# The front of a hybrid mixer: two small pieces of work given out in other projection groups

## The chip, the cores and the metric

The kernel runs on one core of one Trainium2 chip. The time is that of the device for one execution, in microseconds (us). The engines are TensorE (PE in the profile, with its weight loads as PEld), VectorE (DVE), ScalarE (ACT), GpSimd (POOL) and SyncE (SP); SP issues nearly all transfers here.

## The reference, cut to what matters

One decoder layer over 512 tokens of width 1024: an RMS norm, one input projection, whose columns feed a differential attention and an RWKV-7 time mixing, then the output projection, a product-key expert stage and a gated embedding. The change touches what stands at the front of the two mixers:

```python
u = rms_norm(h, norm_mix_g[i]);  z = u @ w_in[i]          # (512, 3328)
# time mixing: shift by one token, then keys, receptances, values, low-rank columns
zs = z_rw + (prev - z_rw) * mu
kk = heads(k * k_k)
kk = kk / jnp.maximum(jnp.sqrt(jnp.sum(kk * kk, axis=-1, keepdims=True)), 1e-12)
# attention: rotation's tables, and lambda
ang = positions[..., None] * inv_freq;  cos, sin = jnp.cos(ang), jnp.sin(ang)
lam = jnp.exp(jnp.sum(lam_q1 * lam_k1)) - jnp.exp(jnp.sum(lam_q2 * lam_k2)) + lam_init
```

## The kernel before

Tokens lie in four blocks of 128 partitions. Every float32 product is made of three matmuls: operands are split in a high part (`whi`, `uhi`, made on ACT, L133) and the rest (`wlo`, `ulo`, made on DVE, L145 where a gain is folded in, L143 elsewhere), and `proj_steps` (L217 to L219) adds high by high, high by rest and rest by high.

The front is a chain of projection groups, each of eight chunks of 128 rows of the weight: the keys "k" (512 columns), the low-rank columns "l" (256), the receptances "r" (512), the values "v" (512), and then the attention's queries, keys and values. `stream` fetches two chunks at a time into `wraw` (three buffers), and the halves of a pair of chunks share one of two buffers, so that ACT can make `whi` of a pair only when PE is done with the pair two before. A chunk is twelve matmuls, three for each block of tokens. When a group is done, `consume` of `shift_group` copies it to `zz` on ACT (L446), SP moves it by one token (L455 to L460), and POOL makes the mix with `mu` in three operations for each block (L461, L462, L464: `zs`).

`rw_keys` makes the normalised keys: the product `kk` on DVE (L475), its square on ACT (L477), the sums (L478), a reciprocal root in small steps on DVE (`rsqrt`, L94 to L103, L481) and four products (L484). `rope_tables` makes the cosine and sine tables from the positions by some 46 operations on tiles of 128x32 on DVE (L355 to L423) and two functions on ACT (L418, L424). `lambdas` makes two products on DVE (L340), an exponential on ACT (L342) and two small steps. After the values, `rw_prepare` starts with the low-rank columns: transposes, the copies `lw` and `lg` on DVE (L502, L504), then the matmuls `plw` and `pla` (L506, L510).

The order on each engine isn't that of the text: a planner goes through the program with its own costs and gives each engine the earliest work in the program's order that it believes to be ready, so that later work fills gaps; each engine then runs its queue strictly in that order. Tiles of a tag (the pages `p2`, 32 of them, hold `mu`, `zs`, `kk`, `zz` of "l" and others) are given out by the planner. `behind(i, first)` adds an edge for the planner alone: `i` stands behind `first` on its engine, without a semaphore. `last_lo`, `last_hi` and `last_z` are the latest `wlo`, `whi` and `zz` at that place in the program. `among` is a table of steps that `proj_steps` calls after the halves of a given chunk have been made and before that chunk's matmuls.

In the kernel before, `rw_keys` is called between the receptances and the values, and `rope_tables` and `lambdas` after the values.

Of the kernel before, what the change touches and what calls it, by code (L numbers as in the profile page):

```python
# [14 lines left out]
OP = mybir.AluOpType  # L15
# [7 lines left out]
RW0 = 1536  # L23
# [24 lines left out]
def bcast_row(ap, n):  # L48
    return bass.AP(tensor=ap.tensor, offset=ap.offset, ap=[[0, 128], [1, n]])
# [7 lines left out]
class Kernel:  # L57
# [274 lines left out]
    def lambdas(self, pool):  # L332
        nc, a = self.nc, self.a
        lam = pool.tile([128, 4, 64], F32, name="lam")
        for i, nme in enumerate(("lam_q1", "lam_k1", "lam_q2", "lam_k2")):
            nc.sync.dma_start(lam[:, i, :], bcast_row(a[nme], 64))
        e = pool.tile([128, 2], F32, name="lame")
        scr = pool.tile([128, 64], F32, name="lams")
        for i in range(2):
            nc.vector.scalar_tensor_tensor(scr, lam[:, 2 * i, :], 1.0, lam[:, 2 * i + 1, :], op0=OP.mult, op1=OP.mult,  # L340
                                           accum_out=e[:, i:i + 1])
        self.behind(nc.scalar.activation(e, e, AF.Exp), self.last_z)  # L342
        self.nlam = pool.tile([128, 1], F32, name="nlam")

        nc.vector.tensor_sub(self.nlam, e[:, 1:2], e[:, 0:1])
        nc.vector.tensor_scalar(self.nlam, self.nlam, -LAM_INIT, None, op0=OP.add)

    def rope_tables(self, pool, tmp):

        nc, a = self.nc, self.a  # L350
        n = NB * 8
        pi32 = tmp.tile([128, NB], I32, name="pi32")
        nc.sync.dma_start(pi32, a["positions"])
        pf = tmp.tile([128, NB], F32, name="posf")
        nc.vector.tensor_copy(pf, pi32)  # L355
        freq = tmp.tile([128, 8], F32, name="freq")
        inv = np.power(np.float32(500000.0), -np.arange(8, dtype=np.float32) * np.float32(2.0) / np.float32(16))
        for j in range(8):
# [6 lines left out]
        def f(name):  # L365
            return tmp.tile([128, n], F32, name=name)
# [52 lines left out]
        w = f("xw")  # L419
# [6 lines left out]
    def p2(self, name, shape=(128, 512), dt=F32):  # L426
        return self.pages.tile(list(shape), dt, name=name, tag="p2", bufs=32)
# [468 lines left out]
    def mixers(self, ocat_pool, psum):  # L896

        tc, nc, a = self.tc, self.nc, self.a
        w = a["w_in"]
        with ExitStack() as ctx:  # L900
# [6 lines left out]
            cpool = self.pool(ctx, "mx_const")  # L907
# [3 lines left out]
            hi = act.tile([128, KC, T], F32R, name="uhi")  # L911
            lo = act.tile([128, KC, T], F32R, name="ulo")
            g = cpool.tile([128, KC], F32, name="g_mix")
# [6 lines left out]
            def columns(k):  # L920

                xt = self.p4("xt", [128, 2, T])
                nc.sync.dma_start(xt, a["xT"][k * 128:(k + 2) * 128, :].rearrange("(k p) t -> p k t", k=2))
                self.split(hi[:, k:k + 2], lo[:, k:k + 2], xt)

            def square(b):
                x = self.p4("xb")
                nc.sync.dma_start(x, a["x"][b * 128:b * 128 + 128, :])
                self.squares(x, x, ssx[:, b:b + 1])

            def row_scales():
                self.rms(rs, ssx)

            p2, p4 = self.p2, self.p4
            zs = {}
            columns(0)
            begin = {0: [lambda: columns(2)], 2: [lambda: columns(4)], 4: [lambda: columns(6)],
                     6: [lambda b=b: square(b) for b in range(NB)] + [lambda: self.mixer_consts(cpool)],
                     7: [row_scales]}
            for tag, c0, n in (("k", 512, 512), ("l", 1536, 256), ("r", 0, 512), ("v", 1024, 512)):  # L940
                z, consume = self.shift_group(rs, (lambda: self.small.tile([128, 256], F32, name="zsl", bufs=NB))
                                              if tag == "l" else (lambda: p2("zs")), c0, n)
                if tag == "v":
                    kk = self.rw_keys(zs["k"])
                self.proj(psum, hi, lo, w, RW0 + c0, n, consume, g=g, among={} if zs else begin)
                zs[tag] = z
                if tag == MARK:
                    self.mark = self.last_hi
            self.rope_tables(cpool, cpool)
            self.lambdas(cpool)  # L950
            zd, qT, kT, vs = {}, {}, [], {}

            def eat_z(b, ps):
# [771 lines left out]
```

## Time and profile before

| | us |
|---|---|
| median of 3 runs | 1800.03 (1797.09 to 1800.13) |
| the profiled execution | 1795.69 |
| its span in the trace | 1794.0 |
| PE busy in it | 1691.8 |
| DVE busy in it | 1397.3 |
| mean granted clock of PE | 0.966 of full speed |

The times are those of one launch; the span is from the first to the last instruction that the profiler recorded. In a row of a timeline stand the start, the duration, the engine, the line of the kernel, the operation and its tiles with their sizes (out<-in), the count where rows were merged, and in brackets how long the engine had been idle and what ended that. [...]

### The profile page before, as it was taken

How to read it: one execution, taken by the hardware profiler on the slowest of the kernel's cores; microseconds unless marked ns; L12 is line 12 of the kernel's file. 1: busy time of each engine (PE TensorE's matmuls, PEld its weight loads, DVE VectorE, ACT ScalarE, POOL GpSimd, SP SyncE). 2: the span in 40 equal slices, each digit the busy share in tenths (PEclk: the TensorE clock that was granted, in tenths of full speed). 3: DMA queues.
4: the chain of work that ended last, by engine and by line, in shares of the span. 5: the costliest groups of instructions: out<-in, count | busy, mean ns of one | idle time of the engine just before them, and what ended most of it. 6: DMA issues, size and time to landing. Idle time of an engine off the chain costs nothing.

```text
span 1794.0 us, 30877 instructions
## 1 busy us (share of the span) xinstructions
PE 1691.8 (94%) x11642; PEld 1447.2 (81%) x11642; DVE 1397.3 (78%) x3004; ACT 751.5 (42%) x1358; POOL 647.3 (36%) x574
## 2 busy tenths in 40 slices
PE   7899978989889879999999999999999999999998
PEld 5767667667677879997777888888999989989986
DVE  5486858774499979878888888888888888888785
ACT  5345523343456654444444333333333333333363
POOL 3460120212278840001111233335545455555520
PEclk9899966899999989999999999999999999999999
DMA  7444353414522434455665677778989898989881
GB/s 230 147 128 118 106 130 87 111 27 165 188 82 81 139 102 132 137 188 198 210 208 190 221 267 235 262 266 299 315 301 316 301 319 301 313 308 315 304 321 47
DMA packets 150426, 363.86 MB, mean 203 GB/s; under 512 B 43922, under 2 KB 58510, under 8 KB 150148
## 3 DMA queue, kind: packets, MB, share of 16 engines
q1 hardware_dynamic: 113412, 227.65, 38.9%
q0 software_dynamic: 36864, 134.23, 22.1%
q8 instruction: 91, 1.49, 0.3%
q14 instruction: 59, 0.48, 0.1%
HBM read 332.61 MB, written 21.36 MB: 197 GB/s over the span
## 4 chain that ended last, share of the span: by engine, by line
PE 67%; DVE 24%; ACT 4%; issue 2%; DMA 2%; POOL 1%; SPq 0%; DVEq 0%; ACTq 0%; POOLq 0%
PE po L1395 22%; PE phid L1253 9%; PE phid L1255 9%; PE phid L1254 8%; PE pg L1364 3%; ACT whi L133 2%; DVE wlo L143 2%; PE acc L217 2%; PE acc L218 2%; PE acc L219 2%; DVE ids L1202 1%; DVE rest L1079 1%; DVE sol_p L630 1%; DVE wlo L145 1%; DVE jj L1352 1%
## 5 line engine op out<-in xcount | busy, mean ns | idle before, releaser
L143 DVE TENSOR_TENSOR wlo<-wraw,whi 128x1024 fp32r<-128x1024 f32 x245 | 299.6, 1223 | 144.7 <-ACT whi L133 144.6
L133 ACT ACTIVATE whi<-wraw 128x1024 fp32r<-128x1024 f32 x276 | 291.4, 1056 | 166.6 <-PE phid L1254 68.5
L1253 PE MATMUL phid<-u2dhi,whi 128*128 128x384 f32 x1024 | 349.1, 341 | 5.7 <-ACT row L1262 5.7
L1255 PE MATMUL phid<-u2dhi,wlo 128*128 128x384 f32 x1024 | 346.1, 338 | 5.5 <-POOL wlo L143 5.5
L1254 PE MATMUL phid<-u2dlo,whi 128*128 128x384 f32 x1024 | 345.6, 338 | 0.0
L1418 POOL DMA_INDIRECT row<-in_peer_u_dram,idx x128 | 190.0, 1485 | 408.0 <-DVE row L1430 219.4
L1418 POOL DMA_INDIRECT row<-in_peer_v_dram,idx x128 | 186.0, 1453 | 276.3 <-DVE h L1434 194.4
L1395 PE MATMUL po<-whi,clo 128*128 128x512 f32 x768 | 243.1, 398 | 1.4
L1395 PE MATMUL po<-whi,chi 128*128 128x512 f32 x768 | 243.3, 398 | 1.2 <-ACT row L1262 1.2
L1395 PE MATMUL po<-wlo,chi 128*128 128x512 f32 x768 | 241.4, 395 | 0.0
L1253 PEld LDWEIGHTS phid<-u2dhi,whi 128*128 128x128 f32 x1024 | 193.5, 189 | 10.8 <-ACT row L1262 6.6
L1255 PEld LDWEIGHTS phid<-u2dhi,wlo 128*128 128x128 f32 x1024 | 193.4, 189 | 6.1 <-POOL wlo L143 6.1
L1254 PEld LDWEIGHTS phid<-u2dlo,whi 128*128 128x128 f32 x1024 | 193.7, 189 | 3.7
L1395 PEld LDWEIGHTS po<-whi,clo 128*128 128x128 f32 x768 | 143.0, 188 | 41.9 <-DVE clo L145 8.7
L1395 PEld LDWEIGHTS po<-wlo,chi 128*128 128x128 f32 x768 | 144.4, 188 | 33.6
L133 ACT ACTIVATE chi<-gelu 128x384 fp32r<-128x384 f32 x128 | 67.3, 526 | 240.6 <-DVE gelu L1372 121.4
L1434 DVE SCALAR_TENSOR_TENSOR h<-row,ids,h 128x1024 f32<-128x1024 f32 x128 | 163.9, 1280 | 1.5
L1395 PEld LDWEIGHTS po<-whi,chi 128*128 128x128 f32 x768 | 140.9, 188 | 25.6 <-ACT row L1262 1.5
L1262 ACT ACTIVATE gelu<-phid 128x384 f32<-128x384 f32 x86 | 42.4, 493 | 266.4 <-PE phid L1255 244.8
L1430 DVE SCALAR_TENSOR_TENSOR row<-row,xn 128x1024 f32<-128x1024 f32 x128 | 153.6, 1219 | 0.0
L143 POOL TENSOR_TENSOR wlo<-wraw,whi 128x1024 fp32r<-128x1024 f32 (+1 forms) x46 | 80.0, 1752 | 111.3 <-ACT whi L133 111.3
L218 PE MATMUL acc<-wlo,uhi 128*128 128x512 f32 (+1 forms) x224 | 89.7, 401 | 10.7 <-DVE wlo L145 10.7
(452 smaller groups left out, 2866.1 us busy)
## 6 DMA issues: line engine op xcount, KB each, us to landing
wraw<-in_peer_uT_dram SPq DMA_DIRECT2D x128, 512.0 KB
wraw<-in_peer_v_dram SPq DMA_DIRECT2D x128, 512.0 KB
wraw<-in_w_in_dram SPq DMA_DIRECT2D x24, 512.0 KB
wraw<-in_peer_w_q_dram SPq DMA_DIRECT2D x16, 512.0 KB
ahead<-row SPq DMA_DIRECT2D x42, 192.0 KB
gelu<-ahead SPq DMA_DIRECT2D x42, 192.0 KB
wraw<-in_w_out_dram SPq DMA_DIRECT2D x8, 512.0 KB
zz<-zz SPq DMA_DIRECT2D x12, 224.0 KB
```

The costliest lines, as they stand in the source:

```text
L133: self.last_hi = nc.scalar.activation(hi, src, AF.Copy, **({} if g is None else {"scale": g}))
L143: self.last_lo = eng.tensor_tensor(lo[s], src[s], hi[s].bitcast(F32), op=OP.subtract)
L218: nc.tensor.matmul(o, hi[:, k, s], wlo, start=False, stop=False)
L1253: nc.tensor.matmul(ps, whi[:, s], hi[:, k, :], start=(k == 0), stop=False)
L1254: nc.tensor.matmul(ps, whi[:, s], lo[:, k, :], start=False, stop=False)
L1255: nc.tensor.matmul(ps, wlo[:, s], hi[:, k, :], start=False, stop=(k == KC - 1))
L1262: nc.scalar.activation(g, ps, AF.Gelu)
L1364: nc.tensor.matmul(ps[:, t], jj[:, t], gi[:, i, t], start=i == 0, stop=i == 1)
L1395: nc.tensor.matmul(outs[b, e], lhs[:, s], rhs[:, 512 * e:512 * e + 512], start=(c == 0 and rhs is vhi and lhs is chi), stop=(c == NKEY - 1 ...
L1418: nc.gpsimd.indirect_dma_start(out=row, out_offset=None, in_=a["peer_u" if kind == "U" else "peer_v"], in_offset=bass.IndirectOffsetOnAxis ...
L1430: nc.vector.scalar_tensor_tensor(row, row, 1.0, xn0, op0=OP.mult, op1=OP.mult, accum_out=hid0[:, k:k + 1])
L1434: nc.vector.scalar_tensor_tensor(acc0, row, hid0[:, k:k + 1], acc0, op0=OP.mult, op1=OP.add)
```

## The change

`rw_keys` is no longer called between the receptances and the values, but inside the receptances' group, after the halves of chunk 4. `rope_tables` and `lambdas` are no longer called after the values, but inside the values' group, after the halves of chunk 1. The first DVE operation of the tables (`posf`) and the two products of lambda are put behind the latest `wlo` at that place, which is that of chunk 1 of the values; before they had no such edge.

```diff
@@ -337,8 +337,8 @@
         e = pool.tile([128, 2], F32, name="lame")
         scr = pool.tile([128, 64], F32, name="lams")
         for i in range(2):
-            nc.vector.scalar_tensor_tensor(scr, lam[:, 2 * i, :], 1.0, lam[:, 2 * i + 1, :], op0=OP.mult, op1=OP.mult,
-                                           accum_out=e[:, i:i + 1])
+            self.behind(nc.vector.scalar_tensor_tensor(scr, lam[:, 2 * i, :], 1.0, lam[:, 2 * i + 1, :], op0=OP.mult,
+                                                       op1=OP.mult, accum_out=e[:, i:i + 1]), self.last_lo)
         self.behind(nc.scalar.activation(e, e, AF.Exp), self.last_z)
         self.nlam = pool.tile([128, 1], F32, name="nlam")
 
@@ -352,7 +352,7 @@
         pi32 = tmp.tile([128, NB], I32, name="pi32")
         nc.sync.dma_start(pi32, a["positions"])
         pf = tmp.tile([128, NB], F32, name="posf")
-        nc.vector.tensor_copy(pf, pi32)
+        self.behind(nc.vector.tensor_copy(pf, pi32), self.last_lo)
         freq = tmp.tile([128, 8], F32, name="freq")
         inv = np.power(np.float32(500000.0), -np.arange(8, dtype=np.float32) * np.float32(2.0) / np.float32(16))
         for j in range(8):
@@ -932,7 +932,7 @@
                 self.rms(rs, ssx)
 
             p2, p4 = self.p2, self.p4
-            zs = {}
+            zs, kk = {}, []
             columns(0)
             begin = {0: [lambda: columns(2)], 2: [lambda: columns(4)], 4: [lambda: columns(6)],
                      6: [lambda b=b: square(b) for b in range(NB)] + [lambda: self.mixer_consts(cpool)],
@@ -940,14 +940,13 @@
             for tag, c0, n in (("k", 512, 512), ("l", 1536, 256), ("r", 0, 512), ("v", 1024, 512)):
                 z, consume = self.shift_group(rs, (lambda: self.small.tile([128, 256], F32, name="zsl", bufs=NB))
                                               if tag == "l" else (lambda: p2("zs")), c0, n)
-                if tag == "v":
-                    kk = self.rw_keys(zs["k"])
-                self.proj(psum, hi, lo, w, RW0 + c0, n, consume, g=g, among={} if zs else begin)
+
+                among = {"k": begin, "r": {4: [lambda: kk.extend(self.rw_keys(zs["k"]))]},
+                         "v": {1: [lambda: self.rope_tables(cpool, cpool), lambda: self.lambdas(cpool)]}}
+                self.proj(psum, hi, lo, w, RW0 + c0, n, consume, g=g, among=among.get(tag, {}))
                 zs[tag] = z
                 if tag == MARK:
                     self.mark = self.last_hi
-            self.rope_tables(cpool, cpool)
-            self.lambdas(cpool)
             zd, qT, kT, vs = {}, {}, [], {}
 
             def eat_z(b, ps):
```

## Rows read from the trace of the kernel before

**Rows 1.** The page, part 1: engine, busy us, share of the span, instructions.

```profile
PE 1691.8 (94%) x11642; PEld 1447.2 (81%) x11642; DVE 1397.3 (78%) x3004; ACT 751.5 (42%) x1358; POOL 647.3 (36%) x574
```

**Rows 2.** PE in order of time: start, us, engine, line, operation, [idle before <-releaser].

```profile
33.42 0.28 PE L217 MATMUL acc<-whi,uhi 128*128 128x256 f32 x1
...
39.22 0.28 PE L217 MATMUL acc<-whi,uhi 128*128 128x256 f32 x1
42.95 0.38 PE L218 MATMUL acc<-wlo,uhi 128*128 128x256 f32 x1 [3.46 <-DVE wlo L145]
...
55.13 0.58 PE L218 MATMUL acc<-wlo,uhi 128*128 128x256 f32 x1 [7.23 <-DVE wlo L145]
...
82.38 0.39 PE L217 MATMUL acc<-whi,uhi 128*128 128x512 f32 x1
...
111.10 1.56 PE L506 MATMUL plw<-w_up,lw 65*128 65x512 f32 x2 [3.97 <-DVE lw L502]
```

**Rows 3.** Stretches of the front: busy us (instructions) by engine, PEclk, DMA share, GB/s.

```profile
43.00:47.00 4.00, 4.00 (x21) 4.00 (x22) 4.00 (x8) 0.91 (x2) 3.84 (x4) 0.57 0.62 193
...
55.20:60.50 5.30, 5.30 (x23) 5.11 (x24) 1.73 (x4) 2.12 (x5) 0.00 (x0) 0.50 0.38 121
...
82.40:104.80 22.40, 22.40 (x98) 17.88 (x97) 17.17 (x15) 9.25 (x16) 18.45 (x12) 1.00 0.46 146
...
111.00:118.50 7.50, 7.40 (x15) 4.66 (x16) 5.38 (x11) 1.46 (x3) 6.66 (x5) 0.54 0.32 81
```

**Rows 4.** DVE in order of time, 31 to 92 us.

```profile
35.81 1.27 DVE L394 TENSOR_SCALAR h<-h 128x32 f32<-128x32 f32 x1
...
42.42 1.89 DVE L145 SCALAR_TENSOR_TENSOR wlo<-wraw,g_mix,whi 128x256 fp32r<-128x256 f32 x2
...
52.15 0.18 DVE L387 SCALAR_TENSOR_TENSOR x<-x0q,x 128x32 f32<-128x32 f32 x1
...
54.59 0.88 DVE L145 SCALAR_TENSOR_TENSOR wlo<-wraw,g_mix,whi 128x256 fp32r<-128x256 f32 x2
...
78.91 1.41 DVE L145 SCALAR_TENSOR_TENSOR wlo<-wraw,g_mix,whi 128x512 fp32r<-128x512 f32 x2 [2.96 <-ACT whi L133]
```

**Rows 5.** POOL in order of time, 20 to 130 us.

```profile
35.59 1.45 POOL L461 TENSOR_TENSOR zz<-zz 128x512 f32<-128x512 f32 x1 [27.27 <-DMA zz<-zz]
...
50.88 1.29 POOL L464 TENSOR_TENSOR zs<-zz 128x512 f32<-128x512 f32 x1
...
85.40 1.29 POOL L461 TENSOR_TENSOR zz<-zz 128x512 f32<-128x512 f32 x1 [12.43 <-DMA zz<-zz]
```

**Rows 6.** DVE from 88 to 114 us: groups by line, then the first in time.

```profile
L145 DVE SCALAR_TENSOR_TENSOR wlo<-wraw,g_mix,whi 128x512 fp32r<-128x512 f32 x6 | 8.8, 1478 | 3.6 <-ACT whi L133 3.6
L475 DVE TENSOR_TENSOR kk<-zs,b_rw_k_k 128x512 f32<-128x512 f32 x4 | 5.9, 1497 | 0.0
L478 DVE TENSOR_REDUCE knr<-ksq 128x8 f32<-128x512 f32 x4 | 2.6, 676 | 0.1
L484 DVE TENSOR_TENSOR kk<-kk,knx 128x512 f32<-128x512 f32 x4 | 2.5, 684 | 0.0
...
91.58 3.46 DVE L475 TENSOR_TENSOR kk<-zs,b_rw_k_k 128x512 f32<-128x512 f32 x2
```

**Rows 7.** SP's issues in order of time, then one of ACT.

```profile
40.22 4.49 SPq L169 DMA_DIRECT2D wraw<-in_w_in_dram  x3
44.76 0.46 SPq L438 DMA_DIRECT2D mu<-in_rw_mu_dram  x1
...
92.11 0.46 SPq L438 DMA_DIRECT2D mu<-in_rw_mu_dram  x1
...
43.32 0.91 ACT L133 ACTIVATE whi<-wraw,g_mix 128x256 fp32r<-128x256 f32 x2 [5.83 <-DMA wraw<-in_w_in_dram]
```

**Rows 8.** ACT in order of time, 100 to 115 us.

```profile
106.15 1.28 ACT L418 ACT_TABLE_LOAD   x1
...
113.11 1.32 ACT L133 ACTIVATE whi<-wraw,g_mix 128x512 fp32r<-128x512 f32 x2
```

## The prediction

> **What bounds the kernel now.** I read the page first: PE is busy for 94% of the span [rows 1], so only its holes are worth anything, and the change lies in the front, before 130 us. So I read that stretch alone: PE in order of time for its holes, then a table by stretches for the clock, then DVE, POOL, ACT and SP in order of time for what fills or ends each hole. Every hole of PE over 1 us between 10 and 130 us is in [rows 2]: 3.46 us and 7.23 us in the low-rank group "l", both ended by DVE's wlo (L145), and 3.97 us at plw, ended by DVE's copy lw (L502). Each is followed by a stretch at a lower granted clock [rows 3]: 0.57 over 4.0 us, 0.50 over 5.3 us and 0.54 over 7.5 us. [...] What such a stretch costs I take as its length times what is missing from 1.00: 1.7, 2.65 and 3.45 us. PE works through all of it, so this is time of the end.
>
> What fills the holes: DVE's queue is in order, and between the wlo of "l" stand the 42 small steps of the rotation's tables, 25 of them between 35.81 and 52.15 us [rows 4]. POOL runs the keys' shift at that time (twelve operations, the first at 35.59, the last until 52.17 us) [rows 5]. Steps of the same 128x32 shape take 1.27 us while POOL runs and 0.18 us after it has stopped; the 13 that come after it take 2.44 us together, up to the wlo at 54.59. In the third hole DVE is at the keys' lengths: twelve steps of rsqrt, one minimum and four products (L484) stand ahead of lw [rows 6].
>
> **What the change removes.** (a) The tables go out of "l". That takes away 3.46 + 1.7 + 7.23 + 2.65 = 15.0 us. Not all returns, for something is late next: the last pair of "l" was fetched at 40.22 us, behind the shift's transfers on SP, and its whi on ACT started on landing, at 43.32 us [rows 7]. PE starts "l" at 33.42 us and the first matmul of chunk 4, 48 matmuls on, at 39.22 [rows 2], so 72 of them (six chunks of twelve at 0.121 us) would be done at 42.1 us; whi and wlo of the last pair are there at about 44.3 us. A hole of 2.2 us stays, with a slow stretch behind it of nothing up to the 1.7 us of the 3.46 us hole; I take half, since 2.2 us lies between no hole and that one. Worth: 15.0 - 2.2 - 0.85 = 11.9 us (bounds 11.1 to 12.8).
>
> (b) The keys' lengths go out of the stretch ahead of lw: 3.97 + 3.45 = 7.4 us. The next thing late there would be whi of the second pair of the queries' group, held to 113.11 us by the tables' three ACT functions [rows 8]; these leave as well. I take 7.4 (bounds 4 to 7.4, the low one if the clock is low there anyway). Will the planner move the keys at all? kk needs zs of the keys, which POOL had at 52.17 us at the latest [rows 5], and stands behind the receptances' last wlo, yet starts at 91.58 us [rows 6]. Beside it the loads of mu (L438), which wait for no data, leave only at 44.76 (for "l") and 92.11 us (for the values), each after the tiles of the group before [rows 7]. Both share the pages p2, so I read that pages are given in the program's order. Before, kk came behind the receptances' zs in that order; now it comes ahead of them, so it can follow the wlo of chunk 4. mu of the values then comes after those zs, with time in hand (the values are multiplied by it after their own consume, past 104.8 us).
>
> **What it adds.** (c) The receptances' group gets, on DVE, four kk at 1.50, four sums at 0.68, some 13 steps at 0.19 and four products at 0.68 us [rows 6]: 6.0 + 2.7 + 2.5 + 2.7 = 13.9 us beside POOL, 10.6 without it (kk then at 0.68 as L484). Queued behind them are the wlo of chunks 5 to 7, for which PE waits. A pair of chunks lasts PE a quarter of a group's 22.4 us [rows 3], 5.6 us, and the wlo are made a pair ahead. From the end of PE's first pair, whi 0.7, wlo of chunk 4 0.9, then kk, sums and wlo of chunk 5 9.6 us, then wlo of chunk 6 0.9: 12.1 us, against PE's need at 11.2. Late by 0.9 at the 1.50 price, early at 0.68; I take 0.5 (0 to 4; a fall of the clock is in the upper bound).
>
> (d) The values' group gets the 42 steps, two lambda products, and on ACT sine, exponential and cosine with three table loads of 1.28 us [rows 8]. The new order adds no semaphore; it makes posf and the products queue behind wlo of chunk 1, and everything after them in the program, so wlo of chunks 2 to 7, stands behind as far as the planner finds them ready. On before's clock, wlo of chunk 1 is done at 80.32 us [rows 4], PE starts the values at 82.38 us [rows 2], and POOL starts the receptances' shift at 85.40 us [rows 5] and is busy with it for 18.5 us [rows 3]. So 5.1 us are free of POOL: less 0.7 for two other small steps, 23 tables' steps at 0.19 (2.44 us for the 13 after POOL's end). The other 19 fall beside POOL at (52.15 - 35.81 - 1.89) / 25 = 0.58 us: 11.0 us; with wlo of chunks 2 and 3 among them (2.3, between the pair beside POOL in "l", 1.89, and two at the 1.48 of [rows 6]) the chain ends at 98.7 us. Chunks 4 and 5 are due at 82.4 + 11.2 = 93.6 us. Late by 5.1, plus 0.7 for the wlo itself, plus a slow stretch as after the 7.23 us hole, 2.65: 8.4 us. Bounds: 0, if the planner puts that wlo among the steps as it did in "l"; 16 if keys delay the start by 3 us so that 16 more steps fall beside POOL (16 x 0.39 = 6.2) and ACT's functions hold the next whi for over 1 us.
>
> (e) At nothing: the load of positions and the four of lambda wait for no one and fill SP where it is idle or waits for a free wraw; without that cover each costs SP some 0.5 us, as the load of mu at 44.76 [rows 7]. The three table loads only move; at the old place they stand in the hole of (b).
>
> [...] Steps of 1.27 us beside POOL and 0.18 us beside none are in [rows 4, 5]. [...]
>
> **The sum.** -11.9 - 7.4 + 0.5 + 8.4 = -10.4 us. The profiled execution took 1795.7 us (span 1794.0), 4.3 below the median of the runs, 1800.0; against it the sum gives 1785.3, and on the runs' scale 1789.6 us. Behind 130 us everything starts from what these groups produce, and PE or DVE is busy throughout, so I let the whole shift pass to the end.
>
> **Rivals.**
> First, the tables find their gap: (d) costs 0 and (c) 0, so -19.3 us, 1781 us. For it: DVE has idle time in that group (17.2 of 22.4 us busy, kk included) [rows 3]. Against: POOL is busy for 18.5 of these 22.4 us.
> Second, the hole moves: the 42 steps meet POOL's shift almost whole, (d) 16 and (c) 2 us: -1.3, 1799 us. For it: the 1.27 us steps. Against: the pair lasts 5.6 us here and half of that in "l".
> Third, the change does not move the keys, since kk waited for something other than pages: -11.9 + 8.4 = -3.5, 1797 us. For it: the planner's reasons stand in no row. Against: the loads of mu.
> Fourth, slower: DVE becomes the bound of both groups. At the prices beside POOL, 16 wlo at 1.48, keys 13.9 and tables and lambda 25 us make 62.6 us where PE needs 44.8: 17.8 us late, and two slow stretches more (5.3): +23.1, against 19.3 gained, +3.8, 1804 us. It decides from 19.3 us of lateness. For it: 1.48 us is the mean that the wlo beside POOL showed [rows 6]. Against: POOL rests between its shifts, so not every step pays.
>
> **How the numbers follow.** Forecast 0.48, first rival 0.17, second 0.13, third 0.10, fourth 0.12. About 0.2% (3.6 us) is what a measurement can tell from no change. Faster by more: forecast, first and a little of the third, 0.68; within: 0.20; slower: 0.12. The forecast's own range is 1784 to 1797 (bounds of (a), (b) and half of those of (d)); to hold 8 in 10 it must reach to the first rival and to the second and part of the fourth: 1781 to 1802.
>
> **What would show it.** Right: no hole by DVE in "l" but one of about 2 us that ends on the last pair's landing; lw free as soon as its transposes are done, and no hole at plw; kk at some 55 us; a hole in the values' group ended by wlo, of 3 to 8 us, with sine after it. Wrong: kk still after the receptances' zs (third); the values' group full (first), or holes in it of over 10 us (second, fourth); holes behind 130 us that before did not have, which the sum leaves out.

## The result, and the profile after

| | before | after |
|---|---|---|
| median | 1800.13 us (1797.09 to 1800.84, 5 runs) | 1789.32 us (1784.86 to 1791.89, 5 runs) |
| ratio after / before | | 0.9937 (0.9926 to 0.9949) |
| the profiled execution, its span | 1795.69, 1794.0 | 1784.86, 1783.2 |

The change takes off 10.8 us by the medians; by the ratio it is 0.63%, with an interval from 0.51% to 0.74%, which is 9.2 to 13.3 us. The prediction was 1789.6 us, within 1781 to 1802. The page's first part, for [rows 1]: PE is busy for 4.2 us less, in a span that is 10.8 us shorter, so more than half of what went are holes.

```profile
PE 1687.6 (95%) x11642; PEld 1442.5 (81%) x11642; DVE 1395.2 (78%) x3004; ACT 749.5 (42%) x1357; POOL 649.4 (36%) x574
```

PE in order of time, for [rows 2]. The group "l" starts at 33.93, the receptances at 47.68, the values at 70.84, their end is the transpose ptl at 103.27.

```profile
33.93 0.28 PE L217 MATMUL acc<-whi,uhi 128*128 128x256 f32 x1
...
44.35 0.74 PE L217 MATMUL acc<-whi,uhi 128*128 128x256 f32 x4 [1.64 <-ACT whi L133]
...
47.68 0.39 PE L217 MATMUL acc<-whi,uhi 128*128 128x512 f32 x1
...
70.84 0.50 PE L217 MATMUL acc<-whi,uhi 128*128 128x512 f32 x1 [0.39 <-ACT zz L446]
72.46 0.50 PE L218 MATMUL acc<-wlo,uhi 128*128 128x512 f32 x1 [1.12 <-DVE wlo L145]
...
85.87 0.49 PE L217 MATMUL acc<-whi,uhi 128*128 128x512 f32 x1 [1.12 <-ACT whi L133]
89.41 0.80 PE L218 MATMUL acc<-wlo,uhi 128*128 128x512 f32 x1 [3.05 <-DVE wlo L145]
...
103.27 0.27 PE L497 MATMUL ptl<-ident,zsl 128*64 128x128 f32 x1
...
104.30 1.09 PE L506 MATMUL plw<-w_up,lw 65*128 65x512 f32 x2
```

The two holes of "l" (3.46 and 7.23 us) have become one of 1.64, and the one ahead of plw (3.97 us) is gone: plw has no bracket. New are 0.39 and 1.12 us at the head of the values, 0.81 us at their chunk 2, and 1.12 and 3.05 us at their chunk 4. The table by stretches, for [rows 3], shows the clock behind them: 1.00 in "l" after its hole, 0.53 for 6.6 us after the holes at chunk 4, then 1.00 again.

```profile
44.40:47.00 2.60, 2.50 (x19) 2.29 (x19) 2.60 (x4) 1.79 (x4) 2.52 (x3) 1.00 0.75 263
...
89.40:96.00 6.60, 6.59 (x16) 5.18 (x17) 5.01 (x3) 0.79 (x2) 6.36 (x5) 0.53 0.45 128
96.00:103.30 7.30, 7.30 (x33) 5.75 (x32) 1.42 (x2) 3.24 (x5) 0.91 (x1) 1.00 0.44 139
```

DVE in order of time, for [rows 4] and [rows 6]:

```profile
55.37 1.22 DVE L475 TENSOR_TENSOR kk<-zs,b_rw_k_k 128x512 f32<-128x512 f32 x1
...
69.25 2.49 DVE L484 TENSOR_TENSOR kk<-kk,knx 128x512 f32<-128x512 f32 x4
71.66 1.41 DVE L145 SCALAR_TENSOR_TENSOR wlo<-wraw,g_mix,whi 128x512 fp32r<-128x512 f32 x2
...
76.51 0.19 DVE L387 SCALAR_TENSOR_TENSOR x<-x0q,x 128x32 f32<-128x32 f32 x1
...
78.99 1.27 DVE L387 SCALAR_TENSOR_TENSOR x<-xrq,x 128x32 f32<-128x32 f32 x1
...
87.53 1.17 DVE L423 TENSOR_SCALAR x<-x 128x32 f32<-128x32 f32 x1
88.62 5.80 DVE L145 SCALAR_TENSOR_TENSOR wlo<-wraw,g_mix,whi 128x512 fp32r<-128x512 f32 x4
```

The keys start at 55.37 instead of 91.58 us and end with L484 at 71.74, just ahead of the first wlo of the values. The tables' steps run from 72.99 at 0.12 to 0.19 us each until POOL starts; the one at 78.99, after it, takes 1.27. ACT and POOL, for [rows 5], [rows 7] and [rows 8]:

```profile
43.79 0.91 ACT L133 ACTIVATE whi<-wraw,g_mix 128x256 fp32r<-128x256 f32 x2 [5.78 <-DMA wraw<-in_w_in_dram]
...
84.98 0.23 ACT L418 ACTIVATE sin<-x 128x32 f32<-128x32 f32 x1 [8.43 <-DVE x L417]
85.11 1.32 ACT L133 ACTIVATE whi<-wraw,g_mix 128x512 fp32r<-128x512 f32 x2
```
```profile
78.67 1.55 POOL L461 TENSOR_TENSOR zz<-zz 128x512 f32<-128x512 f32 x1 [12.05 <-DMA zz<-zz]
```

Sine waits 8.43 us for the last step ahead of it on DVE (L417), and the whi of chunks 4 and 5 stand right behind it. Four more steps (L420 to L423) wait for sine and stand on DVE ahead of the wlo of these chunks.

### The profile page after: what moved, and what is told of

It reads as the page before. It is cut to its first block, busy times and chain, and to the rows that moved or that the text cites. A ratio compares the mean times of both kernels' runs of the same rounds, so it can differ in the third digit from the quotient of the medians.

```text
span 1783.2 us, 30878 instructions
## 1 busy us (share of the span) xinstructions
PE 1687.6 (95%) x11642; PEld 1442.5 (81%) x11642; DVE 1395.2 (78%) x3004; ACT 749.5 (42%) x1357; POOL 649.4 (36%) x574
## 4 chain that ended last, share of the span: by engine, by line
PE 66%; DVE 23%; ACT 5%; issue 2%; DMA 2%; SPq 1%; POOL 1%; DVEq 0%; ACTq 0%; POOLq 0%
PE po L1394 22%; PE phid L1252 9%; PE phid L1254 9%; PE phid L1253 9%; PE pg L1363 3%; ACT whi L133 2%; DVE wlo L143 2%; PE acc L217 1%; PE acc L218 1%; PE acc L219 1%; DVE ids L1201 1%; DVE rest L1078 1%; DVE sol_p L630 1%; DVE jj L1351 1%; DVE si L1076 1%
## 5 line engine op out<-in xcount | busy, mean ns | idle before, releaser
L133 ACT ACTIVATE chi<-gelu 128x384 fp32r<-128x384 f32 x128 | 67.4, 526 | 240.6 <-DVE gelu L1371 121.4
L217 PE MATMUL acc<-whi,uhi 128*128 128x512 f32 (+1 forms) x224 | 88.0, 398 | 12.8 <-ACT whi L133 12.4
```

The source lines that it names most:

```text
L133: self.last_hi = nc.scalar.activation(hi, src, AF.Copy, **({} if g is None else {"scale": g}))
L217: nc.tensor.matmul(o, hi[:, k, s], whi, start=(k == 0), stop=False)
```

## The experiments

Each kernel ran beside the kernel before, whose medians in the three sets were 1799.95 (keys alone to late functions), 1799.51 (short shifts and early fetch) and 1800.52 us (the last four). The table gathers what is used below: the median, and, in the profiled execution, the time from the first matmul of "l" to the first of the receptances, to ptl, to the first block's e_ex on DVE (L517 in the changed kernel) and to the first matmul pwu, where the solve's result comes in. From pwu to the end the profiled executions take 1540 to 1547 us; after and its repetition, the same kernel, differ by 2.5 us there. So the marks tell where a gain lies, and the medians what is left of it; the medians of two kernels that differ by about 2 us or less are not told apart by these runs.

| kernel | median | receptances | ptl | e_ex | pwu |
|---|---|---|---|---|---|
| before | 1800.1 | 26.1 | 71.4 | 92.4 | 218.1 |
| after | 1789.3 | 13.8 | 69.3 | 83.0 | 209.3 |
| after, repeated in the last set | 1789.0 | 15.6 | 70.9 | 84.6 | 211.1 |
| keys alone | 1794.7 | 26.1 | 71.5 | 85.2 | 214.1 |
| tables alone | 1790.3 | 14.7 | 71.8 | 85.5 | 212.4 |
| before, keys' shift short | 1790.8 | 17.2 | 62.0 | 85.1 | 210.3 |
| after, receptances' shift short | 1783.7 | 15.3 | 63.9 | 77.6 | 203.4 |
| keys two chunks earlier | 1787.9 | 14.6 | 67.4 | 81.1 | 207.0 |
| late functions | 1787.6 | 14.7 | 64.2 | 77.9 | 206.9 |
| after, values' shift short | 1787.8 | 14.6 | 70.0 | 82.8 | 208.9 |
| late functions, values' shift short | 1782.3 | 14.9 | 64.5 | 77.2 | 203.0 |
| late functions, early fetch | 1786.7 | 12.8 | 65.0 | 78.7 | 205.7 |
| tables in the keys' group | 1781.9 | 16.4 | 61.9 | 75.5 | 201.5 |
| the same, late mix | 1784.1 | 14.8 | 61.0 | 66.3 | 201.6 |

### Each half alone

Keys alone: the tables stand where they stood before, without the edges of the change.

```diff
-                         "v": {1: [lambda: self.rope_tables(cpool, cpool), lambda: self.lambdas(cpool)]}}
...
+            self.rope_tables(cpool, cpool)
+            self.lambdas(cpool)
```

> The keys' lengths in the receptances' group as in the changed kernel, tables and lambda as before. Theory (parts add up; each hole is paid with the slow stretch behind it): the two holes in "l" stay (DVE, about 3.5 and 7.2 us), the hole at plw goes, the keys cost the receptances about 0.3 us: between the kernel before and this one 6 to 7 us are gained, 1793 to 1794 us. Rival A (the hole at plw belongs to the tables: sine, exponential and cosine on ACT and the steps ahead of them hold DVE or PE there in any case): no gain, 1799 to 1801 us. Rival B (the holes in "l" let the keys be finished for nothing, so the keys' move brings more alone than beside the tables): 1790 us.

1794.74 us, ratio 0.9971 (0.996 to 0.9982): 5.2 us. Tables alone: the keys stand between the receptances and the values again.

```diff
-                among = {"k": begin, "r": {4: [lambda: kk.extend(self.rw_keys(zs["k"]))]},
+                if tag == "v":
+                    kk.extend(self.rw_keys(zs["k"]))
```

> Tables and lambda in the values' group as in the changed kernel, the keys' lengths between receptances and values as before. Theory (parts add up): "l" is 12.4 us shorter, the values' group pays for the tables, and the hole at plw of about 4 us with its slow stretch stays: 1794 to 1797 us, so that e1 and e2 together give the 10.8 us of the whole change. Rival A (the price in the values' group comes from the keys' steps that delay the start of the tables): without keys ahead of them the tables are done before POOL's shift starts, the hole in the values' group is gone: 1787 to 1790 us. Rival B (DVE is the bound of the values' group with keys and tables in it): 1799 us or more.

1790.29 us, ratio 0.995 (0.9936 to 0.9965): 9.7 us by the medians, 9.0 by the ratio. That is not the 1794 to 1797 us that I had expected, and the hole at plw that should have stayed is gone too. Two rows of PE of keys alone, then PE, DVE and ACT of tables alone:

```profile
55.45 0.58 PE L218 MATMUL acc<-wlo,uhi 128*128 128x256 f32 x1 [7.14 <-DVE wlo L145]
...
106.33 1.09 PE L506 MATMUL plw<-w_up,lw 65*128 65x512 f32 x2
```
```profile
86.49 0.79 PE L218 MATMUL acc<-wlo,uhi 128*128 128x512 f32 x1 [9.14 <-DVE wlo L145]
```
```profile
84.59 0.17 DVE L417 TENSOR_SCALAR x<-x 128x32 f32<-128x32 f32 x1
...
84.81 1.62 DVE L145 SCALAR_TENSOR_TENSOR wlo<-wraw,g_mix,whi 128x512 fp32r<-128x512 f32 x1
```
```profile
73.82 0.71 ACT L133 ACTIVATE whi<-wraw,g_mix 128x512 fp32r<-128x512 f32 x1
```

The keys' move takes away the hole at plw and nothing else; the tables' move takes away those of "l". The first rival, that the tables would find free room in the values, did not come true, although its time (1787 to 1790 us) was nearly reached. They start 2.1 us earlier there than in after (posf at 70.86), but so does POOL's shift (76.65), and DVE stands 1.36 us among the first steps, waiting for the load of another constant. The hole is 9.14 us, longer than after's, and it is DVE's order that makes it: the wlo that ends it is that of chunk 2, whose whi was made by 74.53 us, and it stands behind all the steps ahead of sine, the last ten of which ran beside POOL. (In after the wlo of chunks 2 and 3 stand among the steps, at 78.32 and 80.19 us.) The keys come behind that hole (kk from 94.19 us on); lw still stands behind their products, but starts 1.8 us after ptl instead of 5.9, and PE does not wait for it.

The halves' 5.2 and 9.0 to 9.7 us add up to more than the 10.8 of the whole; the intervals (about 2 and 2.6 us to either side) leave open whether that is real. A reason why it may be stands in the marks: the hole at plw is gone in both halves, so its 7.4 us are counted twice, and the longer hole of tables alone takes some back. At e_ex the halves give 7.2 and 6.9 us, the whole 9.4 (7.8 in the repetition); at pwu they give 3.9 and 5.7 us, the whole 8.7 (6.9 in the repetition).

### Is it POOL that makes the steps long?

The kernel before, with the keys' shift cut to its last sum:

```diff
+            if g0 != 512:
                 nc.gpsimd.tensor_tensor(zp[:, :n], zp[:, :n], z[:, :n], op=OP.subtract)
                 nc.gpsimd.tensor_tensor(zp[:, :n], zp[:, :n], mu[:, :n], op=OP.mult)
```

> The kernel before, with the keys' shift on POOL cut to four of its twelve operations: the difference (L461) and the product with mu (L462) of the keys are left out, so the keys are the sum of each row and the one before it. DVE's queue in the front is that of the kernel before. Theory of step (a): the tables' steps in the low-rank group are long because POOL runs beside them. Then most of the 42 cost 0.1 to 0.2 us each, the holes of 3.46 and 7.23 us become one of about 2 us that ends on the landing of the last pair, and the time falls by 8 to 12 us against the kernel before, to about 1790 us; the hole ahead of plw stays. Rival: the steps are in the way by their number and place in DVE's queue, whoever runs beside them. Then both holes stay within 1 us and the time stays within 2 us of before.

1790.80 us, ratio 0.995 (0.9937 to 0.9962). The tables' steps and the wlo of "l" stand on DVE in the same order as before; some of its rows, then PE's holes in "l":

```profile
37.30 1.25 DVE L393 TENSOR_SCALAR h<-x 128x32 f32<-128x32 f32 x1
...
41.88 0.17 DVE L408 SCALAR_TENSOR_TENSOR h2y<-h,h2y 128x32 f32<-128x32 f32 x1
41.98 1.30 DVE L387 SCALAR_TENSOR_TENSOR h1y<-h1q,h1y 128x32 f32<-128x32 f32 x1
43.20 0.18 DVE L387 SCALAR_TENSOR_TENSOR x<-x0q,x 128x32 f32<-128x32 f32 x1
```
```profile
43.96 0.74 PE L217 MATMUL acc<-whi,uhi 128*128 128x256 f32 x4 [1.29 <-ACT whi L133]
...
46.63 0.55 PE L218 MATMUL acc<-wlo,uhi 128*128 128x256 f32 x1 [1.93 <-DVE wlo L145]
```

Only two of the 42 steps are long, those at 37.30 and 41.98, and each falls on one of the four POOL operations that are left (37.17 to 38.52 and 41.96 to 43.23); before, eleven were (1.22 to 1.30 us). 10.7 us of holes have become 3.2, and the time falls by 8.7 us with the steps in the same order (the hole ahead of plw stays, at 5.23 us). The rival, that the steps are in the way by number and place alone, falls: they were in the way because they stood beside POOL.

The same cut, of the receptances' shift in the changed kernel (`g0 != 0`), asks it of the values' group:

> The changed kernel with the receptances' shift on POOL cut to four of its twelve operations (difference and product with mu of the receptances left out), so that POOL is nearly silent while the tables run in the values' group. DVE's and ACT's queues stay as they are. Theory of step (d): the lateness there needs POOL, through the last steps of the tables and through sine, which stands ahead of the next whi on ACT and waits for them; without it the steps end by about 80 us, sine runs before PE asks for the next whi, and the holes of 1.1 and 3.1 us go: 4 to 6 us earlier at the first transpose, of which 1.5 to 3 us are left at the end, 1786 to 1788 us. Rival: the order alone makes the hole (42 steps and the functions ahead of wlo and whi, whoever runs beside them): it stays within 1 us, 1789 us.

1783.73 us, ratio 0.9909 (0.9892 to 0.9925): 5.3 us less than the changed kernel in the same set, and 5.4 to 7.0 us at ptl against its two profiles. PE there, and the four POOL operations that are left:

```profile
86.17 0.50 PE L217 MATMUL acc<-whi,uhi 128*128 128x512 f32 x1 [0.93 <-ACT whi L133]
87.09 0.50 PE L218 MATMUL acc<-wlo,uhi 128*128 128x512 f32 x1 [0.43 <-DVE wlo L145]
```
```profile
79.03 5.71 POOL L465 TENSOR_TENSOR zs<-zz 128x512 f32<-128x512 f32 x4 [12.80 <-DMA zz<-zz]
```

The hole of 3.05 us shrinks to 0.43. Sine is as late as before (85.28), for those four operations hold the last steps ahead of it (one of 1.27 us, then three in 2.75), but the four steps behind it cost 0.18 us each where three of them cost 0.87 to 1.17 in the changed kernel. At the end more was left than the 1.5 to 3 us that I had expected: nothing of the gain was given back.

### Does the order on ACT matter?

Sine, its four steps and cosine are given out behind the halves of the values' chunk 5, sine behind that whi:

```diff
-        self.behind(nc.scalar.activation(self.sin.rearrange("p b j -> p (b j)"), x0, AF.Sin), self.last_z)
+        def functions():
+            self.behind(nc.scalar.activation(self.sin.rearrange("p b j -> p (b j)"), x0, AF.Sin), self.last_hi)
...
+                               5: [lambda: self.functions()]}}
```

> The changed kernel with sine, the four steps between and cosine given out after the halves of chunk 5 of the values, sine behind that whi; the 42 steps of DVE stay where they are. Theory (the hole of 4.7 us has two parts: whi of chunks 4 and 5 held on ACT by sine, and wlo of chunk 4 held on DVE by the four steps that wait for sine): whi starts as PE frees its halves, at some 77 us, wlo of chunk 4 follows the last table step at about 85 us; the hole shrinks to 1 us or less with no slow stretch, 1781 to 1785 us. Rival (the 42 steps beside POOL are the price, ACT only shows it): hole of 4 us or more stays, ended by wlo, 1788 to 1791 us.

Keys two chunks earlier (`"r": {2: [`), which would let the tables start earlier:

> The changed kernel with the keys given out after chunk 2 of the receptances instead of 4; nothing else. Theory (the hole of 4.7 us in the values' group is there because the tables' last steps fall beside POOL's shift, having started 3 us late behind the keys): the keys' products come one wlo earlier, the table steps start about 2 us earlier and fewer than six of them take over 1 us; the hole falls to 2 us or less, 1782 to 1786 us. Rival (the hole comes from the order on ACT, where sine stands ahead of whi of chunks 4 and 5, whenever the tables start): hole and time as in the changed kernel, 1788 to 1791 us.

1787.58 us, ratio 0.9929 (0.9914 to 0.9945), and 1787.92 us, 0.9934 (0.992 to 0.9948). Neither is told from the changed kernel by its time, but the traces differ. ACT with late functions:

```profile
78.47 1.33 ACT L133 ACTIVATE whi<-wraw,g_mix 128x512 fp32r<-128x512 f32 x2 [2.75 <-issue]
```

The whi of chunks 4 and 5 come at 78.47 instead of 85.11 us, their wlo at 85.00 instead of 88.62, and no hole of 1 us is left in the values: 5.1 us at ptl (6.7 against the repetition of after). With the keys earlier only the planner's place for kk moved; L484 still ended at 71.65 and posf started at 72.89 us (72.99 in after), because the reciprocal root stands on DVE behind a wlo whose whi, of the receptances' chunks 6 and 7, a transfer holds until 63.34 us. A large hole in the values stays, but at another place: 3.42 us at chunk 2 and 1.37 at chunk 4.

So there are two kinds of holes. Those at chunk 4 of after need two things at once, POOL beside the last steps and the place of the functions ahead of whi on ACT: taking away either gives 5.1 to 7.0 us at ptl. At chunk 2, whose whi does not stand behind sine, the place of the steps ahead of wlo on DVE is enough for 0.8 us (0.81 in after, where that wlo starts at 78.32, before POOL does, and 0.82 with the receptances' shift short); where the last steps or the wlo itself ran beside POOL it is 2.08 (after, repeated), 3.42 (keys earlier) and 9.14 us (tables alone). That second kind is read from the traces.

### Where the late functions' gain went

At ptl the late functions are 5.1 us ahead of after, at pwu 2.4 (6.7 and 4.2 against the repetition), and by the medians 1.7, which the runs do not tell from nothing. DVE and PE behind the values:

```profile
117.91 1.78 DVE L536 SCALAR_TENSOR_TENSOR zs<-ka,zs 128x512 f32<-128x512 f32 x1
...
121.30 1.75 DVE L145 SCALAR_TENSOR_TENSOR wlo<-wraw,g_mix,whi 128x512 fp32r<-128x512 f32 x1
```
```profile
123.10 0.50 PE L218 MATMUL acc<-wlo,uhi 128*128 128x512 f32 x1 [2.51 <-DVE wlo L145]
```

Four of the first block's products and a wlo run at 1.75 to 1.79 us, beside POOL's shift of the values (until 122.50); in after it is three products. To test it, the values' shift is cut as above (`g0 != 1024`), in the changed kernel and in the late functions:

> The changed kernel with the values' shift on POOL cut in the same way (the difference and the product with mu of the values left out, eight POOL operations of 1.3 us fewer). It stands beside the kernel of the late functions with the same cut, and neither has the computation of the values as the reference has it. Theory: POOL's shift of the values beside the first block's products on DVE costs something here too, but little, since those products come as the shift ends: 1 to 3 us less than the changed kernel, 1786 to 1788 us. Rival (DVE's products there are not held by POOL): no change, 1789 us.

> The kernel of the late functions (sine, four steps and cosine behind the halves of chunk 5 of the values) with the same cut of the values' shift. Theory: what it won in the values' group (4.6 us at the first transpose behind it) was given back because its first block's products on DVE meet POOL's shift of the values; without most of that shift they take 0.7 us each instead of 1.8, the hole of 2.5 us at 120 us goes, and it stands 3.5 to 4.6 us ahead of the changed kernel with the same cut. Rival (the gain is lost further on, by order or by the clock): it stands ahead by 1.7 us or less, as without the cut.

1787.83 us, 0.9934 (0.9922 to 0.9946), and 1782.28 us, 0.991 (0.9897 to 0.9924). The difference between them is 5.5 us, where it was 1.7 with the whole shift. The same product takes 0.68 us, and the hole is gone:

```profile
114.69 0.68 DVE L537 SCALAR_TENSOR_TENSOR zs<-ka,zs 128x512 f32<-128x512 f32 x1
```

The times alone, with intervals of some 2 us to either side, would not carry that; the marks do. From ptl to pwu after and its repetition take 140.0 and 140.2 us, the late functions 142.7, and the two with the cut 138.9 and 138.5. So the 2.6 us that the late functions lose on this way are lost to the next of POOL's shifts.

### The hole that stays in "l"

The late functions, with the transfers of the keys' shift of blocks 2 and 3 behind the fetch of the last pair on SP:

```diff
-                for x in range(NB):
-                    shift(x)
+                for x in range(2 if g0 == 512 else NB):
+                    shift(x)
+                self.rest = lambda: [shift(x, self.fetches[-1]) for x in (2, 3)]
...
+            i = nc.sync.dma_start(zp[1:113, :n], z[0:112, :n])
+            if first is not None:
+                self.behind(i, first)
...
+                "l": {6: [lambda: self.rest()]},
```

> The kernel of the late functions, with the transfers of the keys' shift of blocks 2 and 3 put behind the fetch of the low-rank group's last pair on SP. If the hole of 1.6 us that the changed kernel keeps in that group comes from the fetch standing behind those transfers, it goes, and the receptances start 1.6 us earlier; POOL's shift of the keys then ends some 2 us later, which nobody waits for. Of the time 0 to 1.6 us is left at the end (1786 to 1787.6 us), since DVE's products beside POOL's shift of the values may take it back. Rival (the fetch waited for a free buffer): the hole stays, no change.

1786.69 us, 0.9929 (0.9916 to 0.9942). The fetch leaves SP at 36.15 us, 2.6 us after the start of "l" (with late functions at 41.29, 6.8 us after it), and the hole in "l" is gone; but the next fetches, those of the receptances, now leave behind the moved transfers at 41.61, and PE waits for the first of them:

```profile
46.34 1.20 PE L217 MATMUL acc<-whi,uhi 128*128 128x512 f32 x4 [1.56 <-ACT whi L133]
```

So the cause of the hole was SP's order, as step (a) has it, and the edit moved it one group on. "l" and this hole together take 12.8 us, the shortest of all, but nothing is left of that at ptl (65.0 against 64.2; the holes in the values have grown to 1.27, 1.80 and 1.70 us), and no gain shows in the time.

### A place with DVE free and POOL silent

In the profile of after, DVE waits 3.66 and 4.03 us for whi between 20 and 28.5 us, in the keys' group, and POOL has nothing to do until 35 us. There the steps should cost 0.1 to 0.2 us each, as ahead of POOL in after, with nobody waiting. Sine and cosine go into "l", where ACT waits 5.78 us for the last pair; the four steps between them get a tile of their own and come first.

```diff
+                among = {"k": {**begin, 5: [lambda: self.rope_tables(cpool, cpool)]},
+                         "l": {3: [lambda: self.functions()]},
...
-                         "v": {1: [lambda: self.rope_tables(cpool, cpool), lambda: self.lambdas(cpool)]}}
+                         "v": {1: [lambda: self.lambdas(cpool)]}}
```

> The changed kernel, with the tables' DVE steps given out in the keys' group (after the halves of its chunk 5, where POOL has nothing to do until 35 us and DVE is idle for about 7.7 us between its last wlo), sine and cosine in the low-rank group behind the whi of chunk 3, where ACT waits 5.8 us for the last pair; the four steps between sine and cosine work on a tile of their own and come ahead of both. Lambda stays in the values' group. Theory: the whole cost (d) goes, 10.0 us at the first transpose after the values (as far as wlo of the values then finds DVE free), so that it comes at 96 to 98 us; as with the late functions, 2 to 3 us of that go back to POOL's shift of the values beside the first block's products: 1785 to 1787 us. Rival: the keys' group or the low-rank group gets a new hole, from steps ahead of its wlo or functions ahead of its whi: no gain, 1789 us or more.

1781.85 us (1780.64 to 1782.56, 4 runs), ratio 0.9895 (0.9879 to 0.991). The changed kernel beside it:

> The changed kernel itself, on the same chip and in the same rounds as the three others, as the measure for them: 1788 to 1790.5 us. All theories expect the same of it.

1788.98 us (1786.78 to 1794.10, 6 runs), 0.9939 (0.9924 to 0.9954). So this version beats both, by 18.7 and 7.1 us, and no run of the one reaches the other. DVE's last table step, and the stretch of the values that holds after's two holes (82.40 to 89.40), without one:

```profile
28.50 0.18 DVE L422 TENSOR_SCALAR x<-x 128x32 f32<-128x32 f32 x1
```
```profile
82.40:89.40 7.00, 7.00 (x32) 5.64 (x31) 4.53 (x3) 1.34 (x2) 6.76 (x6) 1.00 0.64 213
```

Here no more is given back to POOL's shift of the values than in after (three products at some 1.78 us in both), where I had expected 2 to 3 us: at ptl it is 7.5 us ahead of after, at pwu 7.8. The shift ends 7.5 us after e_ex here (117.51) and 10.2 us after it with late functions (122.50). In their trace its transfers leave SP only at 98.72, behind a fetch that waits for a free wraw, and the whi that free it stand behind cosine on ACT (91.31); here they leave at 95.16. That reading is from the traces and was not tested by itself.

Last, the same with the load of the values' mu on SP behind the store of the first block's last product, so that eight of POOL's operations come after these products:

```diff
+        last = nc.sync.dma_start(by_row(self.d_kh[b]), kh)
+        if b == 0:
+            self.late(last)
+            nc.sync.dma_start(by_row(self.d_v[b]), v)
```

> The same, and the values' shift put later: its load of mu stands on SP behind the store of the first block's last product (d_kh), so that POOL's product with mu and last sum (eight of the twelve operations) run after that block's products on DVE and not beside them; nothing is left out. Theory: the products take 0.7 us each, as where POOL's operations were left out, and the time falls by up to 4 us more, to 1781 to 1784 us. Rival: the eight operations fall beside other DVE work (the diagonals, the second block's products), or the first block's products with the values (pg) wait for them: the time stays within 2 us of the kernel with the tables in the keys' group, or rises above it.

1784.06 us (1781.94 to 1785.81), 0.9912 (0.9897 to 0.9928): not better, and by the medians 2.2 us worse. All of the products but two are short, at 0.68 us (beside POOL's differences e_in takes 1.22 us and e_ex<-kk,e_ex 1.77). (That e_ex comes 9.3 us earlier is another matter: the planner now puts pcum, which e_ex reads, 4.2 us behind ptl on PE instead of 12.6, so this run changes PE's order as well as POOL's place.) But DVE then waits 5.46 us for whi, and POOL's eight operations fall beside the next wlo and delay the second block's lw:

```profile
127.56 2.89 DVE L145 SCALAR_TENSOR_TENSOR wlo<-wraw,g_mix,whi 128x512 fp32r<-128x512 f32 x2 [3.58 <-ACT whi L133]
130.37 0.41 DVE L524 COPY lw<-ptl 64x256 f32<-64x256 f32 x1
```
```profile
130.92 1.10 PE L528 MATMUL plw<-w_up,lw 65*128 65x512 f32 x2 [1.66 <-DVE lw L524]
```

At pwu nothing is left of it (201.6 against 201.5). The rival held.

## Why the prediction was right, and where its working was not

**(a), the tables out of "l": right, in size and cause.** -11.9 us was predicted; the stretch went from 26.1 to 13.8 us in the profile of after (-12.4), and to 14.6 to 15.6 in the seven other profiles of kernels whose tables had gone from "l" into the values and whose fetches were left alone, so -10.5 to -12.4. The hole that stays is the one foreseen, ended by the last pair's landing, at 1.64 us instead of 2.2. The half of a slow stretch was a guess between none and all, and both occur: after the hole of 1.64 us the clock stayed at 1.00, after one of 1.87 us in the repeated run it was 0.67:

```profile
45.30:50.50 5.20, 4.52 (x24) 4.32 (x25) 5.20 (x5) 2.61 (x6) 5.04 (x4) 0.67 0.64 204
```

**(b), the keys out of the stretch ahead of lw: right.** -7.4 us; e_ex comes 9.4 us earlier from the start of "l" and ptl 2.0, which leaves 7.4. The reading of the pages held too: kk moved to 55.37 us, as forecast. Keys alone gave 7.2 us at e_ex and 5.2 by the medians. Tables alone lost the hole at plw too, so the keys ahead of lw cost PE time only where they end late against ptl.

**(c), the receptances: right for that group.** 22.82 to 23.16 us, +0.3 where +0.5 was predicted; kk took 1.22, 1.23, 0.68 and 0.68 us. But (c) looked no further than chunk 7: in after DVE goes from the keys' L484 to the first wlo of the values without a pause, and PE waits 1.12 us for it, which counts below as a part of (d).

**(d), the values: size nearly right, mechanism half right, and partly by luck.** From 22.40 to 32.43 us, +10.0 where 8.4 was predicted; holes that a wlo ends and a slow stretch behind them (0.53 over 6.6 us) came as described. But the working had errors that cancelled. The steps away from POOL were priced at 0.19 us, the mean of the last 13 of them [rows 4], most of which read the result of the one before. The earlier ones belong, by the names of their tiles, to three chains that alternate, and follow each other every 0.08 to 0.13 us. So with POOL starting at 78.67, 37 of the 42 were done ahead of it, not 23. But of the nine that came after its start, the four behind sine among them, seven cost 0.87 to 1.29 us, not 0.58, which was a mean over long and short steps. The rows of before show why, DVE and then POOL:

```profile
37.12 0.19 DVE L395 TENSOR_TENSOR x<-x,h 128x32 f32<-128x32 f32 x1
37.23 1.28 DVE L405 TENSOR_SCALAR h2y<-h 128x32 f32<-128x32 f32 x1
38.42 0.17 DVE L393 TENSOR_SCALAR h<-x 128x32 f32<-128x32 f32 x1
```
```profile
37.13 1.34 POOL L462 TENSOR_TENSOR zz<-zz,mu 128x512 f32<-128x512 f32 x1
38.55 1.32 POOL L464 TENSOR_TENSOR zs<-zz 128x512 f32<-128x512 f32 x1
```

The long step starts after an operation of POOL has started, and ends 0.04 us after it; the short ones start within some 0.1 us around the change from one operation to the next. In "l", where steps of several chains follow each other closely, one or two short ones passed with most of the long ones. The last steps of the tables wait each for the one before, and in after nearly every one met an operation of its own.

The free stretch ahead of POOL was right by luck: the tables started 2.2 us after PE's first matmul of the values instead of 2.1 us ahead of it, behind the keys, and POOL 7.8 us after it instead of 3.0, mostly since its transfers left SP behind a fetch that left at 73.09 us only; so 5.7 us lay between them, where 5.1 was predicted. And sine was left out of the sum but for the upper bound, and the sign that it would come after the hole failed: it stands ahead of whi of chunks 4 and 5, and four steps that wait for it stand ahead of their wlo. The two changed kernels with a short shift or a later sine show that taking away either of these two takes off half of the +10.0 us or more.

**(e), the loads: at nothing, as said.** No hole of after is ended by one of theirs. Of the three table loads of 1.28 us one went: before, sine, the exponential and cosine followed each other on ACT with a load ahead of each (106.15, 107.69 and 109.21 us); in after the exponential comes ahead of both (loads at 72.52 and 75.27), and there is none ahead of cosine.

**The sum and what it left out.** -10.4 us against -10.8. It let the whole shift pass to the end, and that held here (2.0 us at ptl, 9.4 at e_ex, 8.7 at pwu, 10.8 by the medians). It need not have: the late functions lost 2.6 us of their gain between ptl and pwu. What I had not looked for is that POOL's third shift, of the values, stands beside the first block's products and takes back what the front wins if it comes late.

**The rivals.** The first (the tables find their gap, 1781 us) did not happen where the change put them, and its time was reached by putting them where POOL is silent: 1781.9. The third is out: the keys moved. The second and fourth stand on the right cause, DVE's operations longer beside POOL (steps of 0.87 to 1.30 us where they take 0.16 to 0.19 alone), with too high a price: the hole did move, but at 10 us, not 16. Holes of over 10 us in the values did not show; tables alone came near it with 9.14.

**What was long beside POOL.** The product zs<-ka,zs takes 1.78 us beside POOL's shift (late functions) and 0.68 with most of that shift left out. In [rows 6] the sums L478 take 676 ns in the stretch in which kk takes 1497. Steps with one input tile were long as well (L394, 1.27 us in [rows 4]; L420 and L423, 0.87 and 1.17 us in after). Why an operation is long there no run shows; that it is long because POOL runs beside it, the cut shifts show.

## What to carry to other kernels

Before small steps are moved from one gap to another, look which other engine runs beside each: on DVE the 42 small steps of 128x32 cost some 6 us while POOL rests (tables in the keys' group: 7.8 us from 19.99 to 27.80, 1.7 of them a wlo, the wait for it and a memset), and made a hole of PE of 9.14 us where the last ten met POOL's 128x512 operations (tables alone); the best place was the first group, in which POOL is silent. Where an engine's queue gets an operation that waits for another engine (sine for the last step, 8.43 us in after), count what stands behind it in that queue (there the whi of chunks 4 and 5), and its partners behind those (their wlo). A gain at one mark is not a gain at the end: follow it from mark to mark, for what runs beside the work behind it may take it back (late functions, 2.6 us between ptl and pwu).

## What the hardware showed

- While POOL rests, DVE steps of 128x32 that read the result of the step before follow it by 0.20 to 0.23 us, and steps that do not by 0.08 to 0.13 us (by the starts; the row of each has 0.17 to 0.19 us, so the latter overlap). After, before and the tables in the keys' group agree on it; which step reads which is taken from the names of the tiles.
- Beside POOL's 128x512 operations, which last 1.26 to 1.78 us, a step that starts while one runs, and not within some 0.1 us of the change to the next, ends 0.03 to 0.06 us after it (0.87 to 1.30 us; before and after). Where each step waits for the one before, about one passes for each operation of POOL (in after, three in the 3.88 us from 80.85 on, while POOL goes through three); where steps of several chains alternate, about two (before, 25 steps and two wlo beside POOL's twelve operations from 35.6 to 52.2 us).
- POOL pays as well, but less: its operations last 1.27 to 1.30 us where DVE rests and 1.59 to 1.74 beside DVE's products (late functions, 104 to 122 us).
- What the clock did after holes of nearly one size in the same place of "l": 1.00 after those of 1.64 to 1.75 us (after, late functions, values' shift short, tables alone, keys two chunks earlier), then 0.67 (1.87 us, repeated), 0.62 (1.87 us, late functions with the values' shift short), 0.54 (1.88 us, tables in the keys' group) and 0.64 (2.02 us, short receptances' shift), but 1.00 again after one of 1.89 us (late mix, 44.65 to 48.87 us), so the size alone does not say which. The group's 128x256 matmuls took 0.28 us where the clock was 1.00, and 0.41 us in the slow part of the others (repeated until 49.66 us, values' shift short with late functions until 48.40, short receptances' shift until 48.33). Holes of 0.49 to 0.81 us, four in 20 us (late functions, 78 to 98), left it at 1.00.
